# A hybrid S5 / RG-LRU / GLA block on one core: a new order of the first norm, a moved projection block, an earlier fill and a moved group of rests

## The chip, the cores and the metric

One Trainium2 chip, one core. Input and output are fp32. The time is device microseconds of one launch; the kernel before takes 1577.93 us (median of 3 runs, 1577.77 to 1577.96). The engines are called PE (TensorE, matmuls), DVE (VectorE), ACT (ScalarE), POOL (GpSimd) and SP (SyncE, which only issues DMAs).

## The reference, cut to what matters

```python
mod = split((silu(c) @ ada_w + ada_b), 6);  mod_c = the same of c_ctx
u  = modulate(rms_norm(x, ln1_g), mod[0], mod[1])        # 1024 latent tokens x 1024
uc = modulate(rms_norm(ctx, ln1_g), mod_c[0], mod_c[1])  # 256 context tokens x 1024
zl, zc = split(u @ w_in), split(uc @ w_in)               # 1024 x 5408
s5  = S5 scan (256 channels, two directions), gelu, GLU
lru = RG-LRU scan (256 channels, two directions, short conv), times gelu(g)
gla = chunked GLA: 4 heads, q, k of 64, v of 128, chunks of 64, two directions, RMSNorm, times silu(g)
m = sig(g0)*(s5 @ w_br_s5) + sig(g1)*(lru @ w_br_lru) + sig(g2)*(gla @ w_br_gla)
h = x + mod[2] * (m @ w_out)
u = modulate(rms_norm(h, ln2_g), mod[3], mod[4])
hid = dwconv3(u @ w_up)                                  # 1024 x 5632
h = h + mod[5] * ((silu(gate) * val) @ w_down)           # 2816 -> 1024
out = rms_norm(h, final_g)
```

The context goes only through the projection and starts the scans of the latent tokens.

## The kernel before, in words

Activations lie transposed: a tile is 128 channels by 512 or 1024 tokens. Each fp32 product is three matmuls of fp32r operands: high times high, rest times high, high times rest. So every operand is split: its high part is a rounded copy (`wh`, `uh`, `y0h`; mostly ACT) and its rest is the difference to that copy (`wl`, `ul`, `y0l`; DVE or POOL).

The work goes through these stages in time:

- **Start** (list `START`, L87, runs the small functions of class `Start`, L330 to L446). `x`, `sq`, `sa` load and square the eight tiles of x and add up the squares, for token half j = 0 or 1; `rs` sums over channels on PE (L285), `re`, `rp` give the reciprocal root (`rp` is the POOL power at L408), `rb` broadcasts it by PE (L279), `rc` copies it. `a` loads a piece of the adaLN weights, `ar` multiplies a row of eight such pieces (64 matmuls, L316), `at`, `ac`, `am` turn the row into shift and scale of two channel tiles. `un`, `u`, `ul` scale a tile by norm and scale (DVE, L320), add the shift and round (ACT, L323) and take the rest (DVE, L326). `g`, `gh`, `gl` load and split the first weights. `m1` and `m2` are the matmuls of three column blocks with the high part (L434, L435) and the rest (L441); `mz` the last of them. Each list entry issues in the order of the list on every engine.
- **The stream.** `proj_stream` (L762) is a generator of all further projection matmuls in the order in which they are to run. A block of 128 columns on the latent tokens (`lat`) is 48 matmuls of 128x512 in 8 steps of two rows of tokens, stored by the `out_rows` functions. `fill(us)` (L868) takes matmuls from the stream until their summed cost reaches the given number; `F(name)` takes the number from the table `FILL` (L62). The mixers' own matmuls stand between such calls, so the stream fills the time in which a mixer waits. Blocks of the stream share two PSUM buffers each of `ma` and `mb`; ACT or DVE copies them out (the v blocks at L746).
- **LRU, S5, GLU** (L950 to L1260), then **four GLA heads** (class `Head`, L1294; driver at L1488). Of the heads, number 0 makes its decays (L1304 to L1323, DVE and ACT), and then PE transposes (L1347). After the last head `fill(1e9)` (L1531) empties the stream; its last blocks are the gated products, whose gates are added at L826 and L827.
- **Merge** (L1540 to L1580): the heads' output is written to DRAM as `yosp` (L1434), read back as `yr` in four tiles through two buffers (`wide_in`, L1549), split into `y0h`, `y0l` to `y3h`, `y3l`, and multiplied with the branch weights in eight products of 24 matmuls (L290 to L292). Weights come through `wblock`: two raw buffers `wr`, three `wh`, three `wl`.
- **Output projection, residual, second norm**, then the **up projection** in pairs of hidden blocks by a Strassen-like scheme (class `Pair`, L1629): products p1 to p7 of the four quarters of the activation and of sums of them. At the turn from the norm to the pairs (L1790 to L1925) the operand differences T1 to T4 and the quarter B22 are made tile by tile: `sub` (difference, L1831), `hi` (ACT copy, L1834), `lo` (rest, L1837). `units(k)` issues the products 5, 7 and 6 of both first pairs for tile k; p3 multiplies with B22, p4 with T4; `c57` and `z57` add earlier products up before p3 and p4 write to the same PSUM banks. The order of DVE, ACT, POOL and PE is by hand there.
- **Down projection** and the final norm.

The order of PE is as the code is written (`manual_schedule`). In the start and at the turn the other engines are by hand too; elsewhere a scheduler orders them, SP included.

Of the kernel before, what the change touches and what calls it, by code (L numbers as in the profile page):

```python
# [12 lines left out]
OP = mybir.AluOpType  # L13
# [7 lines left out]
KT = 8  # L21
# [16 lines left out]
def _parts(v, bits, n):  # L38
    out = []
    for _ in range(n):  # L40
# [69 lines left out]
def tile_kernel(tc, I, out, dbg=None):  # L110
# [154 lines left out]
    def t0(shape, tag, bufs=1):  # L265
        return p0_.tile(list(shape), F32, name=nm("t0"), tag=tag, bufs=bufs)
# [64 lines left out]
    class Start:  # L331
# [65 lines left out]
        @staticmethod
        def rs(j):
# [482 lines left out]
    def F(name):  # L881
        fill(next(fills[name]))
# [612 lines left out]
    G.memset(Tm, 0.0)  # L1495
    for h in range(4):
        if h == 0:
            F("gtr")
            head.transposed()
            F("gds")  # L1500
            head.states()
        nxt = Head(h + 1) if h < 3 else None
        head.scores(0)

        if nxt:
            with tc.issue_after(head.last.ins):
# [827 lines left out]
```

## Time and profile before

| | |
|---|---|
| median of 3 runs | 1577.93 us |
| profiled execution | 1578.69 us |
| its span, first to last instruction | 1576.6 us |
| PE busy | 1513.6 us, 96% of the span |
| DVE busy | 1096.1 us, 70% |
| ACT busy | 772.3 us, 49% |
| POOL busy | 414.6 us, 26% |
| mean granted TensorE clock | 0.985 |

Busy time is time in which an engine executes. PE is the busiest by far; the span less its busy time is its idle time. The clock is granted at two levels, 2.4 GHz (1.00) and 1.2 GHz (0.50), and a mean between them tells how much of a stretch ran at the lower one. A 128x512 matmul follows its predecessor by 0.23 us at the higher level and by 0.43 us at the lower. A "wait" is idle time of an engine just before an instruction, with the engine and line that released it.

### The profile page before, as it was taken

To read this page: it belongs to the slowest core of one execution; us is meant where nothing else is said; L and a number is where in the kernel's file an instruction comes from. 1 tells how busy PE (TensorE), PEld (TensorE's weight loads), DVE (VectorE), ACT (ScalarE), POOL (GpSimd) and SP (SyncE) were. 2 spreads that over 40 slices of the span, in tenths; PEclk is the share of its full clock that TensorE was granted. 3 is DMA by queue.
4 is the path that set the end of the run, shared out by engine and by line. 5 is a ranking of instruction groups with operands and counts; after the bars stand their busy time and mean duration, and the time that the engine had idled before them with its cause. 6 is when DMAs were issued, how large, how long until landed. Compare 5 with 4: busy or idle time off the path is not lost. (4 is left out here: it accounts for less than half of the span.)

```text
span 1576.6 us, 21571 instructions
## 1 busy us (share of the span) xinstructions
PE 1513.6 (96%) x8144; PEld 1248.9 (79%) x8144; DVE 1096.1 (70%) x1645; ACT 772.3 (49%) x1223; POOL 414.6 (26%) x266
## 2 busy tenths in 40 slices
PE   5999989999996999999999989999999999999997
PEld 4788768877885888888888867778888888878887
DVE  3624379999858434642451899888888888899962
ACT  4523776785534543441332565444444444544661
POOL 2313210011124222222236335333333333000032
PEclk9999999999998999999999999999999999999998
DMA  9764533332224244131574411222222223964303
GB/s 327 256 213 132 187 129 105 117 101 59 59 67 134 77 135 148 70 88 63 172 239 145 141 60 54 94 81 80 81 81 83 93 92 109 371 240 141 101 20 107
DMA packets 93865, 199.04 MB, mean 126 GB/s; under 512 B 13505, under 2 KB 34881, under 8 KB 93633
## 3 DMA queue, kind: packets, MB, share of 16 engines
q1 hardware_dynamic: 82048, 181.75, 34.3%
q10 hardware_dynamic: 11712, 15.91, 2.9%
q8 instruction: 64, 1.05, 0.3%
q14 instruction: 41, 0.33, 0.1%
HBM read 159.11 MB, written 38.52 MB: 125 GB/s over the span
## 5 line engine op out<-in xcount | busy, mean ns | idle before, releaser
L221 POOL TENSOR_TENSOR wl<-wr,wh 128x1024 fp32r<-128x1024 f32 (+1 forms) x78 | 164.2, 2105 | 477.1 <-ACT wh L220 432.8
L220 ACT CAST wh<-wr 128x1024 fp32r<-128x1024 f32 (+2 forms) x87 | 77.1, 891 | 146.2 <-issue 41.3
L221 POOL TENSOR_TENSOR wp<-tmp,wp 128x512 fp32r<-128x512 f32 x44 | 75.2, 1726 | 217.6 <-ACT wp L220 217.6
L534 PE MATMUL ma<-uh,wh 128*128 128x512 f32 x272 | 116.9, 430 | 0.7 <-ACT pt L809 0.7
L534 PE MATMUL mb<-uh,wh 128*128 128x512 f32 x272 | 106.7, 392 | 0.0
L536 PE MATMUL ma<-ul,wh 128*128 128x512 f32 x272 | 106.7, 392 | 0.0
L536 PE MATMUL mb<-ul,wh 128*128 128x512 f32 x272 | 106.7, 392 | 0.0
L538 PE MATMUL mb<-uh,wl 128*128 128x512 f32 x272 | 106.2, 391 | 0.0
L538 PE MATMUL ma<-uh,wl 128*128 128x512 f32 x272 | 105.9, 389 | 0.0
L220 ACT CAST wp<-tmp 128x512 fp32r<-128x512 f32 x78 | 46.5, 619 | 91.4 <-DVE tmp L1648 91.2
L1714 DVE SCALAR_TENSOR_TENSOR ca<-gv,vec,ca 128x1023 f32<-128x1023 f32 (+2 forms) x66 | 62.2, 967 | 23.8 <-ACT ca L1706 23.6
L220 ACT CAST wp<-hd 128x512 fp32r<-128x512 f32 x88 | 52.8, 618 | 49.4 <-PE bkd L2023 26.3
L220 ACT CAST wp<-wr 128x512 fp32r<-128x512 f32 x97 | 58.2, 620 | 32.5 <-DMA wr<-in_wdn_dram 17.1
L1717 DVE SCALAR_TENSOR_TENSOR ca<-gv,vec,ca 128x1023 f32<-128x1023 f32 (+2 forms) x66 | 71.1, 1100 | 0.1
L1378 DVE SCALAR_TENSOR_TENSOR gl<-gl,gl 128x128 f32<-128x128 f32 x72 | 31.2, 433 | 53.1 <-ACT gl L1376 35.6
L534 PEld LDWEIGHTS ma<-uh,wh 128*128 128x128 f32 x272 | 51.3, 189 | 15.4 <-issue 5.2
L221 DVE TENSOR_TENSOR wp<-hd,wp 128x512 fp32r<-128x512 f32 x88 | 60.8, 708 | 1.2 <-ACT wp L220 1.0
L538 PEld LDWEIGHTS ma<-uh,wl 128*128 128x128 f32 x272 | 51.2, 188 | 11.3
L536 PEld LDWEIGHTS ma<-ul,wh 128*128 128x128 f32 x272 | 51.2, 188 | 11.3
L536 PEld LDWEIGHTS mb<-ul,wh 128*128 128x128 f32 x272 | 51.2, 188 | 11.2
L538 PEld LDWEIGHTS mb<-uh,wl 128*128 128x128 f32 x272 | 51.1, 188 | 11.4
L534 PEld LDWEIGHTS mb<-uh,wh 128*128 128x128 f32 x272 | 51.4, 189 | 9.6 <-issue 1.4
(643 smaller groups left out, 4606.3 us busy)
## 6 DMA issues: line engine op xcount, KB each, us to landing
wa<-in_ada_dram SPq DMA_DIRECT2D x96, 256.0 KB
wr<-in_wup_dram SPq DMA_DIRECT2D x46, 512.0 KB
wr<-in_win_dram SPq DMA_DIRECT2D x40, 512.0 KB
wr<-in_wdn_dram SPq DMA_DIRECT2D x22, 512.0 KB
hd<-hid SPq DMA_DIRECT2D x22, 512.0 KB
hid<-ca SPq DMA_DIRECT2D x21, 512.0 KB
wr<-in_wout_dram SPq DMA_DIRECT2D x16, 512.0 KB
tmp<-in_wdn_dram SPq DMA_DIRECT2D x22, 256.0 KB
```

The source lines that it names most:

```text
L220: S.copy(h, src)
L221: lo.tensor_tensor(l, src, f32(h), OP.subtract)
L534: PE.matmul(p[j], h[:, kk], uh[j][:, k], start=f, stop=False)
L536: PE.matmul(p[j], h[:, kk], ul[j][:, k], start=False, stop=False)
L538: PE.matmul(p[j], l[:, kk], uh[j][:, k], start=False, stop=e)
L1378: self.last = V.scalar_tensor_tensor(Sd[:, step], Sd[:, step - 1], self.dec[:, step:step + 1], Sd[:, step], OP.mult, OP.add)
L1714: V.scalar_tensor_tensor(a[:, t0_ + 1:t0_ + 1 + n1], x[:, o:o + n1], fw[0], a[:, t0_ + 1:t0_ + 1 + n1], OP.mult, OP.add)
L1717: V.scalar_tensor_tensor(a[:, t0_ + c - 1:t0_ + n - 1], x[:, o + c:o + n], fw[2], a[:, t0_ + c - 1:t0_ + n - 1], OP.mult, OP.add)
```

## The change

It has four parts.

1. `START` has a new order. The row of adaLN weights is split: its first six pieces are multiplied as soon as they are there, for row 0 ahead of the norm's broadcast, and the last two later. `u(0,0)` and `u(1,0)` stand ahead of the later squares of the second half. The rows 1 to 3 of the weights come earlier among `m1` and `m2`. Three adds of squares go from POOL to DVE, and the third square has a buffer of its own.
2. In the stream, the second q block (`qsp[1]`, 8 steps, 48 matmuls) goes from ahead of the context blocks to behind the first v steps, just ahead of the steps of z.
3. A new cost `gtr0` of 13.0 is filled from the stream ahead of head 0's transposes. It takes 60 matmuls (10 steps); so many fewer are left behind the last head.
4. At the turn, the last two copies and the four rests of B22 go from behind the difference work to right behind the last rest of T2, the rests from POOL to DVE. q[1].p3 goes ahead of q[0].p4 with its gate and output.

```diff
-ONPOOL = [('sq', 2, 1), ('sq', 4, 1), ('sq', 6, 1)]
...
+        'gtr0': [13.0],
...
-    def ada_rows(r, p):
-        for k, w in enumerate(ada.pop(r)):
+    def ada_rows(r, p, k0=0, k1=KT):
+        for k in range(k0, k1):
+            w = ada[r][k]
...
-                t = sqs[k, j] = t0([128, 512], "sq", 3)
+                t = sqs[k, j] = t0([128, 512], "sq" if k != 2 else "sqp", 3 if k != 2 else 1)
...
-            (G if ("sq", k, j) in ONPOOL else V).tensor_tensor(accs1[j], accs1[j], sqs[k, j], OP.add)
+            V.tensor_tensor(accs1[j], accs1[j], sqs[k, j], OP.add)
...
-        wsrc.extend([win[i] for i in (35, 36, 37, 0, 5, 6, 3, 4)] + vsrc)
+        wsrc.extend([win[i] for i in (35, 36, 37, 0, 5, 3, 4)] + vsrc + [win[6]])
...
-        for b in range(2):
-            yield from lat(lambda p: out_rows(p, qsp[b]))
+        yield from lat(lambda p: out_rows(p, qsp[0]))
         for b in range(2):
             yield from ctx(lambda p: out_rows([p], ksp[b]))
         yield from v_steps([0, 1])
+        yield from lat(lambda p: out_rows(p, qsp[1]))
         yield from z_steps()
...
         if h == 0:
+            F("gtr0")
             F("gtr")
             head.transposed()
...
     lo(2, 3)
+    hi(5, 2); hi(5, 3)
+    for k in range(4):
+        lo(5, k)
     units(3)
...
-    hi(5, 2); hi(5, 3)
     for k in range(4):
-        lo(5, k, G)
         sub(4, k)
...
     nxt.sums((7, 3))
+    q[1].p3()
     q[0].p4()
     q[0].gate()
     q[0].out()
-    q[1].p3()
     q[1].p4()
```

On ACT in the start, where L391 (L392 after) are squares, L323 (L324) the first two `u` of half 0, and `t_139` the broadcast norm, there stood before:

```order
L416 COPY t_139<-sm_131 128x512
L377 CAST wh_137<-wr_202 128x256
L391 ACTIVATE t_243<-x_89 128x512
L391 ACTIVATE t_247<-x_90 128x512
L391 ACTIVATE t_253<-x_91 128x512
L391 ACTIVATE t_257<-x_92 128x512
L391 ACTIVATE t_264<-x_93 128x512
L391 ACTIVATE t_268<-x_94 128x512
L391 ACTIVATE t_272<-x_95 128x512
L323 ACTIVATE uh_109<-x_89,mods 128x512
L323 ACTIVATE uh_109<-x_90,mods 128x512
L391 ACTIVATE t_286<-x_96 128x512
```

and now:

```order
L378 CAST wh_137<-wr_222 128x256
L392 ACTIVATE t_233<-x_89 128x512
L392 ACTIVATE t_237<-x_90 128x512
L426 COPY t_139<-sm_131 128x512
L392 ACTIVATE t_251<-x_91 128x512
L324 ACTIVATE uh_109<-x_89,mods 128x512
L324 ACTIVATE uh_109<-x_90,mods 128x512
L392 ACTIVATE t_273<-x_92 128x512
L392 ACTIVATE t_276<-x_93 128x512
L392 ACTIVATE t_283<-x_94 128x512
```

The two `u` stood behind seven squares of the second half; now they stand behind three.

On SP around the last head's output, where `wr` are raw branch weights for the merge, `acc` a weight piece for the up projection and `tg` stored products, there stood before:

```order
L211 DMA wr_6774<-in_wbr_dram 128x256
L1434 DMA yosp<-gl_6512 128x1024
L211 DMA wr_6892<-in_wbr_dram 128x512
L1863 DMA acc_8093<-in_wup_dram 128x512
L1549 DMA yr_6904<-yosp 128x1024
L1549 DMA yr_6908<-yosp 128x1024
L1549 DMA tg_6925<-tsp 128x1024
L1549 DMA tg_6964<-tsp 128x1024
L1549 DMA yr_6912<-yosp 128x1024
L211 DMA wr_6898<-in_wbr_dram 128x512
L1549 DMA yr_6916<-yosp 128x1024
```

and now:

```order
L211 DMA wr_6759<-in_wbr_dram 128x256
L211 DMA wr_6892<-in_wbr_dram 128x512
L211 DMA wr_6898<-in_wbr_dram 128x512
L211 DMA wr_6951<-in_wbr_dram 128x512
L1444 DMA yosp<-gl_6596 128x1024
L1874 DMA acc_8093<-in_wup_dram 128x512
L1560 DMA yr_6904<-yosp 128x1024
L1560 DMA yr_6908<-yosp 128x1024
L1560 DMA tg_6925<-tsp 128x1024
L1560 DMA tg_6964<-tsp 128x1024
L1560 DMA yr_6912<-yosp 128x1024
L1560 DMA yr_6916<-yosp 128x1024
```

`yosp` stood ahead of all three weight loads of the merge; now it stands behind them. The last two `yr` have no weight load between them any more.

At the turn POOL had, before:

```order
L221 TENSOR_TENSOR wp_8044<-tmp_8011,wp_8044 128x512
L221 TENSOR_TENSOR wp_8212<-pt_7868,wp_8212 128x512
L221 TENSOR_TENSOR wp_8215<-acc_8093,wp_8215 128x512
L1837 TENSOR_TENSOR B22l<-h_7281,B22h 128x512
L1837 TENSOR_TENSOR B22l<-h_7283,B22h 128x512
L1837 TENSOR_TENSOR B22l<-h_7285,B22h 128x512
L1837 TENSOR_TENSOR B22l<-h_7287,B22h 128x512
L221 TENSOR_TENSOR wp_8265<-pt_8015,wp_8265 128x512
```

and now DVE has, where `wr_8099` begins the sums of the third pair's weights:

```order
L1848 TENSOR_TENSOR T3l<-h_7279,T3h 128x512
L1848 TENSOR_TENSOR T2l<-h_7279,T2h 128x512
L1848 TENSOR_TENSOR B22l<-h_7281,B22h 128x512
L1848 TENSOR_TENSOR B22l<-h_7283,B22h 128x512
L1848 TENSOR_TENSOR B22l<-h_7285,B22h 128x512
L1848 TENSOR_TENSOR B22l<-h_7287,B22h 128x512
L1659 TENSOR_TENSOR tmp_8194<-wr_8099 128x512
L1659 TENSOR_TENSOR tmp_8196<-tmp_8194,wr_8097 128x512
L221 TENSOR_TENSOR wp_8198<-wr_8097,wp_8198 128x512
L221 TENSOR_TENSOR wp_8201<-tmp_8196,wp_8201 128x512
```

The four rests of B22 stood on POOL behind two rests of weights; now they stand on DVE between the rests of T2 and those sums, and POOL has nothing in their place.

## Rows read from the trace of the kernel before

**Rows 1.** The page: busy us, share of the span, instructions.

```profile
PE 1513.6 (96%) x8144; PEld 1248.9 (79%) x8144; DVE 1096.1 (70%) x1645; ACT 772.3 (49%) x1223; POOL 414.6 (26%) x266
```

**Rows 2.** Waits of PE: who waited for whom, us in total, times, longest.

```profile
PE sm L1347 <- DVE gl L1323: 12.6, 1, 12.6
PE ma L434 <- ACT uh L323: 4.9, 1, 4.9
PE mb L711 <- ACT pt L746: 4.8, 1, 4.8
...
PE sm L1260 <- DVE s L1245: 1.7, 2, 1.3
```

**Rows 3.** Windows: busy us of the engines in a stretch, clock, DMA share, GB/s.

```profile
20.00:40.00 20.00, 14.52 (x196) 12.06 (x187) 9.45 (x20) 6.95 (x14) 6.91 (x7) 0.83 0.91 323
40.00:60.00 20.00, 19.07 (x139) 15.36 (x140) 19.93 (x30) 10.04 (x18) 8.65 (x7) 1.00 0.95 342
200.00:220.00 20.00, 15.22 (x85) 11.28 (x84) 18.30 (x15) 14.31 (x17) 2.14 (x1) 0.83 0.59 198
```

**Rows 4.** Timeline of PE from 12 to 40 us: start, duration, line, idle before, releaser.

```profile
15.85 2.07 PE L279 MATMUL sm<-con,t 128*128 128x128 f32 x8 [1.35 <-POOL t L408]
17.85 3.64 PE L316 MATMUL sm<-wa,c 128*32 128x128 f32 x64
27.26 0.80 PE L434 MATMUL ma<-uh,wh 128*128 128x512 f32 x1 [4.86 <-ACT uh L323]
...
34.74 1.95 PE L316 MATMUL sm<-wa,c 128*32 128x128 f32 x64
```

**Rows 5.** Timeline of ACT from 19 to 33 us.

```profile
26.50 1.32 ACT L323 ACTIVATE uh<-x,mods 128x512 fp32r<-128x512 f32 x2
```

**Rows 6.** Timeline of ACT, then of PE, from 204 to 222 us.

```profile
215.06 0.57 ACT L746 COPY pt<-mb 128x512 f32<-128x512 f32 x1
...
215.68 0.69 PE L711 MATMUL mb<-uh,tmp 128*64 128x512 f32 x1 [4.78 <-ACT pt L746]
```

**Rows 7.** Timeline of PE from 494 to 516 us.

```profile
496.70 0.39 PE L538 MATMUL mb<-uh,wl 128*128 128x512 f32 x1
509.74 2.39 PE L1347 MATMUL sm<-con,gl 128*128 128x128 f32 x10 [12.65 <-DVE gl L1323]
511.78 0.77 PE L534 MATMUL ma<-uh,wh 128*128 128x512 f32 x1
...
```

**Rows 8.** Timeline of SP, DVE and PE from 738 to 778 us.

```profile
740.17 1.95 PE L279 MATMUL sm<-con,gl 128*128 128x128 f32 x16
...
744.71 0.33 SPq L1434 DMA_DIRECT2D yosp<-gl  x1
...
747.83 0.90 SPq L1549 DMA_DIRECT2D yr<-yosp  x2
...
754.42 1.23 DVE L221 TENSOR_TENSOR y0l<-yr,y0h 128x1024 fp32r<-128x1024 f32 x1 [7.81 <-ACT y0h L220]
...
758.17 0.37 SPq L1549 DMA_DIRECT2D yr<-yosp  x1
...
764.79 1.23 DVE L221 TENSOR_TENSOR y3l<-yr,y3h 128x1024 fp32r<-128x1024 f32 x1 [2.12 <-ACT y3h L220]
...
770.78 0.39 PE L290 MATMUL mm<-y0h,wh 128*128 128x512 f32 x1
```

**Rows 9.** Window of half a us, the last with data behind the issue of yosp.

```profile
746.50:747.00 0.50, 0.50 (x4) 0.41 (x3) 0.11 (x1) 0.00 (x0) 0.44 (x1) 1.00 0.62 246
```

**Rows 10.** Timeline of POOL, DVE and PE at the turn, 930 to 962 us.

```profile
938.58 0.68 DVE L221 TENSOR_TENSOR wp<-wr,wp 128x512 fp32r<-128x512 f32 x1
...
942.94 6.84 POOL L1837 TENSOR_TENSOR B22l<-h,B22h 128x512 fp32r<-128x512 f32 x4
...
945.15 1.78 DVE L1837 TENSOR_TENSOR T4l<-h,T4h 128x512 fp32r<-128x512 f32 x1
...
953.48 0.47 PE L853 MATMUL bkd<-T4h,wp 128*128 128x512 f32 x1 [3.15 <-DVE gv L1688]
```

More of the change, by code (lines that the diff above doesn't have):

```diff
@@ L85 @@
 ENGS = {mybir.EngineType.DVE, mybir.EngineType.Pool, mybir.EngineType.Activation, mybir.EngineType.SP}
-ONPOOL = [('sq', 2, 1), ('sq', 4, 1), ('sq', 6, 1)]
-START = [('x', 0, 0), ('sq', 0, 0), ('x', 1, 0), ('sq', 1, 0), ('x', 2, 0), ('sq', 2, 0), ('sa', 1, 0), ('x', 3, 0), ('sq', 3, 0), ('sa', 2, 0), ('x', 4, 0), ('sq', 4, 0), ('sa', 3, 0), ('x', 5, 0), ('sq', 5, 0), ('sa', 4, 0), ('x', 6, 0), ('sq', 6, 0), ('sa', 5, 0), ('x', 7, 0), ('sq', 7, 0), ('sa', 6, 0), ('sa', 7, 0), ('rs', 0), ('re', 0), ('rp', 0), ('rb', 0), ('a', 0, 0), ('a', 0, 1), ('a', 0, 2), ('a', 0, 3), ('a', 0, 4), ('a', 0, 5), ('a', 0, 6), ('a', 0, 7), ('g', 0), ('gh', 0, 0), ('gh', 0, 1), ('ar', 0), ('gl', 0, 0), ('rc', 0), ('gl', 0, 1), ('gh', 0, 2), ('x', 0, 1), ('sq', 0, 1), ('gl', 0, 2), ('x', 1, 1), ('sq', 1, 1), ('at', 0), ('ac', 0), ('x', 2, 1), ('sq', 2, 1), ('sa', 1, 1), ('x', 3, 1), ('sq', 3, 1), ('am', 0), ('sa', 2, 1), ('x', 4, 1), ('sq', 4, 1), ('un', 0, 0), ('x', 5, 1), ('sq', 5, 1), ('un', 1, 0), ('x', 6, 1), ('sq', 6, 1), ('u', 0, 0), ('sa', 3, 1), ('u', 1, 0), ('ul', 0, 0), ('m1', 0, 0), ('sa', 4, 1), ('x', 7, 1), ('sq', 7, 1), ('ul', 1, 0), ('sa', 5, 1), ('m2', 0, 0), ('m1', 1, 0), ('sa', 6, 1), ('sa', 7, 1), ('m2', 1, 0), ('rs', 1), ('a', 1, 0), ('a', 1, 1), ('a', 1, 2), ('a', 1, 3), ('a', 1, 4), ('a', 1, 5), ('a', 1, 6), ('a', 1, 7), ('g', 1), ('gh', 1, 0), ('ar', 1), ('re', 1), ('gh', 1, 1), ('rp', 1), ('gh', 1, 2), ('gl', 1, 0), ('rb', 1), ('at', 1), ('gl', 1, 1), ('gl', 1, 2), ('ac', 1), ('rc', 1), ('am', 1), ('un', 0, 1), ('un', 1, 1), ('u', 0, 1), ('a', 2, 0), ('a', 2, 1), ('a', 2, 2), ('a', 2, 3), ('a', 2, 4), ('a', 2, 5), ('a', 2, 6), ('a', 2, 7), ('ar', 2), ('un', 2, 0), ('u', 1, 1), ('ul', 0, 1), ('g', 2), ('gh', 2, 0), ('u', 2, 0), ('gl', 2, 0), ('m1', 0, 1), ('ul', 1, 1), ('gh', 2, 1), ('gh', 2, 2), ('at', 2), ('gl', 2, 1), ('ul', 2, 0), ('ac', 2), ('gl', 2, 2), ('un', 3, 0), ('m2', 0, 1), ('m1', 1, 1), ('am', 2), ('u', 3, 0), ('un', 2, 1), ('ul', 3, 0), ('m1', 2, 0), ('u', 2, 1), ('un', 3, 1), ('a', 3, 0), ('a', 3, 1), ('a', 3, 2), ('a', 3, 3), ('a', 3, 4), ('a', 3, 5), ('a', 3, 6), ('a', 3, 7), ('ar', 3), ('ul', 2, 1), ('u', 3, 1), ('un', 4, 0), ('g', 3), ('gh', 3, 0), ('gh', 3, 1), ('gl', 3, 0), ('ul', 3, 1), ('gh', 3, 2), ('m2', 1, 1), ('u', 4, 0), ('gl', 3, 1), ('at', 3), ('un', 5, 0), ('m2', 2, 0), ('gl', 3, 2), ('ul', 4, 0), ('ac', 3), ('u', 5, 0), ('m1', 3, 0), ('am', 3), ('ul', 5, 0), ('m1', 2, 1), ('un', 4, 1), ('un', 5, 1), ('u', 4, 1), ('m2', 3, 0), ('un', 6, 0), ('u', 5, 1), ('m2', 2, 1), ('ul', 4, 1), ('u', 6, 0), ('m1', 3, 1), ('ul', 5, 1), ('ul', 6, 0), ('m1', 4, 0), ('un', 7, 0), ('un', 6, 1), ('m2', 3, 1), ('u', 7, 0), ('un', 7, 1), ('m2', 4, 0), ('u', 6, 1), ('ul', 7, 0), ('m1', 5, 0), ('u', 7, 1), ('ul', 6, 1), ('m1', 4, 1), ('ul', 7, 1), ('m2', 5, 0), ('m2', 4, 1), ('m1', 5, 1), ('m1', 6, 0), ('m2', 5, 1), ('m2', 6, 0), ('m1', 6, 1), ('m2', 6, 1), ('mz',)]
@@ new lines @@
+START = [('x', 0, 0), ('sq', 0, 0), ('x', 1, 0), ('sq', 1, 0), ('x', 2, 0), ('sq', 2, 0), ('sa', 1, 0), ('x', 3, 0), ('sq', 3, 0), ('sa', 2, 0), ('x', 4, 0), ('sq', 4, 0), ('sa', 3, 0), ('x', 5, 0), ('sq', 5, 0), ('sa', 4, 0), ('x', 6, 0), ('sq', 6, 0), ('sa', 5, 0), ('x', 7, 0), ('sq', 7, 0), ('sa', 6, 0), ('sa', 7, 0), ('rs', 0), ('a', 0, 0), ('a', 0, 1), ('a', 0, 2), ('a', 0, 3), ('a', 0, 4), ('a', 0, 5), ('ar', 0, 0, 6), ('re', 0), ('rp', 0), ('a', 0, 6), ('a', 0, 7), ('g', 0), ('gh', 0, 0), ('rb', 0), ('gh', 0, 1), ('gl', 0, 0), ('gh', 0, 2), ('x', 0, 1), ('sq', 0, 1), ('gl', 0, 1), ('x', 1, 1), ('sq', 1, 1), ('gl', 0, 2), ('ar', 0, 6, 8), ('rc', 0), ('sa', 1, 1), ('x', 2, 1), ('sq', 2, 1), ('at', 0), ('ac', 0), ('sa', 2, 1), ('am', 0), ('un', 0, 0), ('un', 1, 0), ('u', 0, 0), ('u', 1, 0), ('ul', 0, 0), ('m1', 0, 0), ('ul', 1, 0), ('x', 3, 1), ('sq', 3, 1), ('x', 4, 1), ('sq', 4, 1), ('sa', 3, 1), ('m2', 0, 0), ('x', 5, 1), ('sq', 5, 1), ('m1', 1, 0), ('sa', 4, 1), ('x', 6, 1), ('sq', 6, 1), ('sa', 5, 1), ('x', 7, 1), ('sq', 7, 1), ('a', 1, 0), ('a', 1, 1), ('a', 1, 2), ('a', 1, 3), ('a', 1, 4), ('a', 1, 5), ('ar', 1, 0, 6), ('sa', 6, 1), ('sa', 7, 1), ('m2', 1, 0), ('a', 1, 6), ('a', 1, 7), ('g', 1), ('gh', 1, 0), ('gh', 1, 1), ('gl', 1, 0), ('ar', 1, 6, 8), ('gh', 1, 2), ('rs', 1), ('at', 1), ('gl', 1, 1), ('gl', 1, 2), ('ac', 1), ('re', 1), ('rp', 1), ('am', 1), ('a', 2, 0), ('a', 2, 1), ('a', 2, 2), ('a', 2, 3), ('a', 2, 4), ('a', 2, 5), ('ar', 2, 0, 6), ('un', 2, 0), ('un', 3, 0), ('u', 2, 0), ('rb', 1), ('u', 3, 0), ('ul', 2, 0), ('a', 2, 6), ('a', 2, 7), ('g', 2), ('gh', 2, 0), ('ul', 3, 0), ('gh', 2, 1), ('gl', 2, 0), ('gh', 2, 2), ('ar', 2, 6, 8), ('rc', 1), ('gl', 2, 1), ('m1', 2, 0), ('at', 2), ('un', 0, 1), ('gl', 2, 2), ('un', 1, 1), ('u', 0, 1), ('ac', 2), ('m2', 2, 0), ('un', 2, 1), ('u', 1, 1), ('a', 3, 0), ('a', 3, 1), ('a', 3, 2), ('a', 3, 3), ('a', 3, 4), ('a', 3, 5), ('ar', 3, 0, 6), ('am', 2), ('u', 2, 1), ('ul', 0, 1), ('m1', 0, 1), ('ul', 1, 1), ('ul', 2, 1), ('a', 3, 6), ('a', 3, 7), ('g', 3), ('gh', 3, 0), ('gh', 3, 1), ('ar', 3, 6, 8), ('gl', 3, 0), ('un', 3, 1), ('gh', 3, 2), ('m2', 0, 1), ('gl', 3, 1), ('at', 3), ('u', 3, 1), ('un', 4, 0), ('m1', 1, 1), ('gl', 3, 2), ('ul', 3, 1), ('u', 4, 0), ('ac', 3), ('un', 5, 0), ('m2', 1, 1), ('am', 3), ('u', 5, 0), ('m1', 3, 0), ('ul', 4, 0), ('ul', 5, 0), ('m1', 2, 1), ('un', 4, 1), ('un', 5, 1), ('u', 4, 1), ('m2', 3, 0), ('un', 6, 0), ('u', 5, 1), ('m2', 2, 1), ('ul', 4, 1), ('u', 6, 0), ('m1', 3, 1), ('ul', 5, 1), ('ul', 6, 0), ('m1', 4, 0), ('un', 7, 0), ('m2', 3, 1), ('un', 6, 1), ('u', 7, 0), ('m2', 4, 0), ('un', 7, 1), ('u', 6, 1), ('m1', 5, 0), ('ul', 7, 0), ('u', 7, 1), ('ul', 6, 1), ('m1', 4, 1), ('ul', 7, 1), ('m2', 5, 0), ('m2', 4, 1), ('m1', 5, 1), ('m1', 6, 0), ('m2', 5, 1), ('m2', 6, 0), ('m1', 6, 1), ('m2', 6, 1), ('mz',)]
@@ L340, in ar @@
         @staticmethod
-        def ar(r):
-            ada_rows(r, psm[:, r * 128:(r + 1) * 128])
+        def ar(r, k0, k1):
+            ada_rows(r, psm[:, r * 128:(r + 1) * 128], k0, k1)
         @staticmethod
@@ L394, in sa, with sp, sf @@
         def sa(k, j):
-            (G if ("sq", k, j) in ONPOOL else V).tensor_tensor(accs1[j], accs1[j], sqs[k, j], OP.add)
+            V.tensor_tensor(accs1[j], accs1[j], sqs[k, j], OP.add)
+        @staticmethod
+        def sp(k, j):
+            G.tensor_tensor(sqs[2, j], sqs[2, j], sqs[k, j], OP.add)
+        @staticmethod
+        def sf(j):
+            Start.sa(2, j)
         @staticmethod
```

## The prediction

> **What bounds the kernel now.** I read the busy table first, then PE's waits, then the windows around the longest of them, and last the timelines inside those windows. PE is busy 1513.6 us of a span of 1576.6 us [rows 1], so 63 us of idle time, and the time that matmuls lose at the lower clock, are all that an edit of the order can win. The change adds no matmul and takes none away. PE's waits name the places that it touches: 12.6 us ahead of head 0's transposes, 4.9 us ahead of the first `m1`, 4.8 us in z [rows 2], and at the turn 3.15 us on PSUM buffer `bkd` [rows 10]. The clock costs time beside each: 0.83 of full speed in the windows 20 to 40 and 200 to 220 us [rows 3]. So I cost four parts apart, each at its own stage, against the profiled execution's 1578.69 us (2.1 us more than its span, 0.76 us above the median of 1577.93).
>
> **A. The start.** Before, the broadcast waits 1.35 us for POOL's power and ends at 17.9 us; the row of adaLN weights runs behind it to 21.5 us; the first `m1` begins at 27.26 us after 4.86 us of waiting [rows 4]. What it waits for is `u` on ACT at 26.50, which follows squares of the second half, some of them fed by POOL adds [rows 5]. After, the row's first six pieces (six eighths of 3.64, 2.7 us) begin right behind the sums at 14.5 and cover the power; the broadcast follows to 19.3, the last two pieces (0.9 us) to 20.2. The steps between row and `un` took 2.4 us before and the two `u` no longer stand behind four of the squares, so I put the first `m1` at about 23.2: 4.1 us earlier. Behind it PE's work is the same. A further 1.4 us I expect from the later rows, which now stand among `m1` and `m2`: at full clock such a row takes 1.95 us [rows 4] and its slots for loads come free sooner with less to wait for. That gives 5.5. Against it DVE is 19.93 of 20 us busy from 40 to 60 us [rows 3] and gets three more adds (some 2 us), though it has 10 us free from 20 to 40. I take -5, with bounds of -1 (only the broadcast's wait goes, everything else ends with the loads) and -7 (all of 4.86 and 1.35, and the clock rises sooner).
>
> **B. The moved q block.** The first matmul of z into the second `mb` buffer waits 4.78 us for ACT's copy of the last v block, which comes at 215.06, queued behind ACT's LRU work; the window has a clock of 0.83 [rows 3, 6]. At 0.43 us apart in place of 0.23, the some 4.8 us of matmuls behind the wait lose about 2.3 us. After, 48 matmuls (10.9 us) stand between the v copies and z, so the copy is long done. What is late next: z's second buffer then waits for the q block's own copies, which stand behind ACT's same chain; I find between 0 and 1.5 us for it, and at worst the whole 4.8. The full gain would be 7.1. I take -4, because LRU's chain on DVE (18.30 of 20 us busy from 200 to 220) must follow if PE is not to wait for it later; bounds 0 and -7.
>
> **E. The fill ahead of head 0.** 126 matmuls of the stream run from 742.1 to 770.78 [rows 8], 0.2277 us each, so 60 are 13.66 us. PE's work ends at 497.09 and the transposes begin at 509.74 [rows 7], 12.65 us later. So the wait is covered, with 1.0 us over; the transposes (10 in 2.04 us) and the first five matmuls behind them run at the lower clock before, and cost 2 us less at the higher. Net the transposes' end is about 1.0 us earlier, and 13.66 us of stream are gone from the end: -14.7 if nothing follows.
>
> Something does follow. Let T be 742.1, the end of the last broadcast [rows 8]. Before, the first merge begins at T+28.7 and its 24 matmuls end at T+34.2; y3's rest is ready at 766.02, T+23.9, so it waits for nothing. After, 66 matmuls (15.05 us) are left, and the merge could begin at T+15. Its operands can't: `yosp` is issued at T+2.6 before, and three weight loads now stand ahead of it on SP, the last of which needs the first one's slot; I put it at T+3.75. The first `yr` was issued 3.1 us behind `yosp` [rows 8]. Data of that write were moving until about 746.9, 2.2 us behind its issue [rows 9], so the read comes 2.2 to 3.1 us behind it, at T+5.95 to T+6.85. From `yr` to the end of y0's rest took 7.8 us, and to that of y3's 18.2, of which 1.1 was a weight load ahead of the last `yr` that is now gone: y0 at T+14.7, y2 about T+21.5, y3 at T+23.1 to T+24. A quarter of a merge product is 1.37 us. The first two run on time, the third waits 3.7 us, the fourth ends at T+24.5 at best, and at T+27.8 with the later read and the lower clock behind the wait. Against T+34.2 that is -6.4 to -9.7, with head 0's -1.0 it is -7.4 to -10.7. I take -8; the outer bounds are -5 and -14.7.
>
> The trace can't say which ended the wait of `yr`, the write's end or the queue. The Trainium skill, "DMA: Bandwidth & Descriptors", on where a transfer's fixed cost goes, says a transfer's semaphore fires only when its last byte is confirmed, some 2.0 us plus bytes at 436 GB/s; for 512 KB that is an estimate of 3.2 us, and the trace's 3.1 agrees. By that rule the read comes at T+6.95, and E is near -7.5; by the queue alone, at T+4.5, it would be near -10.
>
> **C and D. The turn.** POOL makes the four rests of B22 from 942.94 in 6.84 us. Beside them four DVE operations took 1.78 each, such as a rest of T4 at 945.15; the same size takes 0.68 otherwise [rows 10]. On DVE the four rests cost 4 x 0.6 (spacing of such operations) = 2.4 us, and save up to 4 x 1.1 = 4.4; the net of -2 moves up q[0]'s last sum, whose absence makes PE wait 3.15 us ahead of p4, and half clock follows. The 2.4 us come ahead of the third pair's sums, so its weights are that much later. With q[1].p3 (12 matmuls, 2.7 us) ahead of q[0].p4, PE has work in that wait if q[1]'s own sums and weights are ready; POOL makes those, and is freed earlier. I find about 1.4 us of wait left in place of 3.15. I take -2; bounds 0 (DVE, which runs without a gap beside these rests, hands the 2.4 us on to PE) and -4.5.
>
> **The sum.** -5 -4 -8 -2 = -19: 1578.69 - 19 = 1559.7 in the profiled execution's terms, 1559 in the median's. The bounds add to -6 and -33.
>
> **The rivals.**
>
> - *The merge gives E back.* The stream runs dry at T+15 and PE waits for y2, y3 and then the merge's weights, which SP issues only behind the `yr`; the half clock stretches the products. For it: y3 is 8.9 us behind the merge's earliest start. Against it: two weights stand ahead of `yosp`, and before the merge ran without a gap. E is then 0: 1567.
> - *DVE sets the pace.* In the stages behind the start and behind z, DVE is 18 to 20 of 20 us busy [rows 3], and neither A nor B takes anything from it. Then A and B vanish into waits for DVE: -10, 1568. Against it: PE waits on DVE nowhere between z and head 0 for more than 1.3 us at once, in S5 at L1260 [rows 2], so DVE has some room there.
> - *Slower: SP holds `yosp`.* The third weight load waits for the slot of the first, freed by POOL's rest, which needs a free `wl` among three that the stream's blocks use. If that comes only when the stream's last block ends (T+15), `yosp` goes out at T+17.4, `yr` at T+20.5, y3 is ready at T+37.6, and the first merge ends at T+39, with the lower clock about T+41.5 in place of T+34.2: E is +6.3. With the other parts at their low ends (-1) that is +5: 1583. It decides from the point where the load waits past T+14. For it: the scheduler put the loads ahead. Against it: the slot's block is used up at about T+1.4.
> - *The change doesn't bite.* Each wait finds another releaser at the same time (loads in the start, ACT's copies in z, head 0's decays later because ACT and DVE copy out the filled blocks): within 3 us of 1578.
>
> **How the numbers follow.** What a measurement can tell from no change is 0.2%, 3.2 us. Forecast 0.59; merge gives E back 0.14; DVE sets the pace 0.14; SP holds `yosp` 0.07, of which slower 0.06 and faster 0.01; no bite 0.05, which is the same; anything else slower 0.01. Faster is then 0.59 + 0.14 + 0.14 + 0.01 = 0.88, the same 0.05, slower 0.07. The range is 1547 (12 below the forecast, with most parts near their best bound) to 1573 (14 above: either middle rival and a further 5 us, or a part of both).
>
> **What would show it.** The wait at L1347 gone, and PE at a clock of 1.00 from 490 to 515 us. The first `m1` at about 23 us and the start's end five to six us earlier. The wait at L711 gone or under 1.5 us. A new wait of 3 to 7 us in the first merge (L290 or L291, on y2 or y3). At the turn, rests of T4 at 0.68 and a `bkd` wait near 1.4. Wrong would be: a merge that waits over 10 us, `yosp` later than T+6, or a stage between 70 and 480 us that gets a DVE wait as long as what the start gained.

## The result, and the profile after

The changed kernel takes 1553.55 us (median of 4 runs, 1552.12 to 1554.15) against 1577.95 us: a ratio of 0.9843, interval 0.9826 to 0.9860, so 24.4 us faster. A second set of runs gave 1552.99 us and 0.9846 (0.9833 to 0.9860). Forecast were 1559 us and a range of 1547 to 1573. Below, a kernel's distance to the changed one is its ratio less 0.9845 (between the two ratios just named), times 1577.7 us. Each ratio's interval is about ±0.0014, or ±2.2 us, and a distance holds two of them, so about ±3 us.

First the page, to set beside [rows 1] (engines' busy time and share):

```profile
PE 1508.3 (97%) x8144; PEld 1240.7 (80%) x8144; DVE 1090.7 (70%) x1652; ACT 773.6 (50%) x1223; POOL 398.5 (26%) x259
```

The span is 1552.4 us. PE is idle for 44 us in place of 63, and its busy time is 5 us less with the same 8144 matmuls: the mean clock is 0.996 in place of 0.985.

The waits of PE after (who waited for whom, us in total, times, longest), to set beside [rows 2]:

```profile
...
PE ma L444 <- ACT uh L324: 2.0, 1, 2.0
PE sm L317 <- DMA wa<-in_ada_dram: 1.7, 7, 0.3
...
PE bkd L863 <- DVE gv L1699: 1.4, 1, 1.4
...
PE mm L290 <- ACT y2h L220: 1.3, 1, 1.3
...
PE mm L291 <- DVE y2l L221: 0.8, 1, 0.8
```

The wait ahead of head 0 and the one in z are gone, the first `m1`'s has shrunk to 2.0 us. New are PE's waits for weight pieces in the start and for y2 in the merge. The wait of 1.4 us on `bkd` is not the one at the turn: it comes at 990.9 us, in a later pair.

The windows after (busy us by engine, then clock, DMA share, GB/s), the first three beside [rows 3]:

```profile
20.00:40.00 20.00, 16.38 (x217) 11.43 (x217) 14.36 (x27) 9.20 (x18) 6.54 (x7) 1.00 1.05 387
40.00:60.00 20.00, 19.81 (x107) 15.91 (x108) 18.52 (x30) 10.18 (x19) 5.96 (x4) 1.00 1.00 349
200.00:220.00 20.00, 19.50 (x143) 13.16 (x142) 13.35 (x11) 18.25 (x24) 2.40 (x1) 1.00 0.32 116
480.00:520.00 40.00, 39.85 (x219) 32.79 (x218) 22.68 (x23) 19.41 (x34) 16.35 (x7) 1.00 0.24 83
748.00:756.00 8.00, 6.47 (x19) 4.53 (x20) 3.85 (x4) 2.29 (x3) 1.12 (x1) 0.79 0.26 96
```

The clock is 1.00 where it was 0.83; of the stretches shown, only the first merge's lost it.

Where did the time come from? The same matmuls found in both traces tell how much earlier each place comes: behind the start -4.2 us, behind z and from there to head 0 -11.7, at the last head's broadcast -12.5, behind the first merge -21.9, at 935 us (behind the turn's third products) -25.2, at the end -24.8. So by these two executions the parts are A -4.2, B -7.5, E -10.2 (-0.9 at head 0, -9.4 at the merge) and C with D -2.9.

The timeline of PE in the start after (start, duration, line, idle before and releaser), beside [rows 4]:

```profile
14.24 2.79 PE L317 MATMUL sm<-wa,c 128*32 128x128 f32 x48
16.96 1.30 PE L279 MATMUL sm<-con,t 128*128 128x128 f32 x8
18.18 0.64 PE L317 MATMUL sm<-wa,c 128*32 128x128 f32 x16
20.08 0.39 PE L352 MATMUL sm<-con,t 128*128 128x8 f32 x2 [1.25 <-DVE t L348]
22.49 0.50 PE L444 MATMUL ma<-uh,wh 128*128 128x512 f32 x1 [2.02 <-ACT uh L324]
...
30.95 0.42 PE L317 MATMUL sm<-wa,c 128*32 128x128 f32 x8 [0.25 <-DMA wa<-in_ada_dram]
31.62 0.43 PE L317 MATMUL sm<-wa,c 128*32 128x128 f32 x8 [0.25 <-DMA wa<-in_ada_dram]
...
35.74 0.50 PE L444 MATMUL ma<-uh,wh 128*128 128x512 f32 x1
```

Six pieces run in the time of POOL's power, as intended, and the first `m1` is at 22.49, 4.8 us earlier. Behind it the lead first grows to 7.1 us, because these matmuls follow each other 0.23 us apart, and before 0.43. But the third row's pieces come one by one, 0.67 us apart, and behind the start 4.2 us are left.

At head 0 (timeline of PE, beside [rows 7]) the transposes follow the stream without a gap and at the higher clock:

```profile
498.95 0.39 PE L548 MATMUL mb<-uh,wl 128*128 128x512 f32 x1
499.18 1.25 PE L1357 MATMUL sm<-con,gl 128*128 128x128 f32 x10
500.19 0.48 PE L544 MATMUL ma<-uh,wh 128*128 128x512 f32 x1
```

The tail after, from the timeline of all engines, beside [rows 8]:

```profile
727.63 1.95 PE L279 MATMUL sm<-con,gl 128*128 128x128 f32 x16
...
733.16 0.33 SPq L1444 DMA_DIRECT2D yosp<-gl  x1
...
734.00 1.55 SPq L1560 DMA_DIRECT2D yr<-yosp  x2
...
741.61 1.05 ACT L220 CAST y0h<-yr 128x1024 fp32r<-128x1024 f32 x1 [10.40 <-DMA yr<-yosp]
...
742.69 1.23 DVE L221 TENSOR_TENSOR y0l<-yr,y0h 128x1024 fp32r<-128x1024 f32 x1 [7.63 <-ACT y0h L220]
...
743.94 1.56 SPq L1560 DMA_DIRECT2D yr<-yosp  x2
...
744.50 0.39 PE L290 MATMUL mm<-y0h,wh 128*128 128x512 f32 x1
...
748.68 0.50 PE L290 MATMUL mm<-y2h,wh 128*128 128x512 f32 x1 [1.27 <-ACT y2h L220]
...
750.00 0.50 PE L291 MATMUL mm<-y2l,wh 128*128 128x512 f32 x1 [0.82 <-DVE y2l L221]
...
750.74 1.23 DVE L221 TENSOR_TENSOR y3l<-yr,y3h 128x1024 fp32r<-128x1024 f32 x1 [0.80 <-ACT y3h L220]
...
753.89 0.63 PE L292 MATMUL mm<-y3h,wl 128*128 128x512 f32 x1
...
754.32 0.51 PE L290 MATMUL mm<-y0h,wh 128*128 128x512 f32 x1
```

With T at 729.58, `yosp` goes out at T+3.6, the merge begins at T+14.9, y2's rest is ready at T+20.4 and y3's at T+22.4, and the first product ends at T+24.7 in place of T+34.2.

At the turn (timeline of all engines, beside [rows 10]) the rests of B22 cost 2.49 us and those of T4 0.68 each, in place of 1.78:

```profile
915.36 2.49 DVE L1848 TENSOR_TENSOR B22l<-h,B22h 128x512 fp32r<-128x512 f32 x4
...
924.62 0.68 DVE L1848 TENSOR_TENSOR T4l<-h,T4h 128x512 fp32r<-128x512 f32 x1
...
929.33 0.49 PE L863 MATMUL bkc<-B22h,wp 128*128 128x512 f32 x1 [0.94 <-ACT gv L1695]
...
930.10 0.50 PE L864 MATMUL bkc<-B22h,wp 128*128 128x512 f32 x1 [0.28 <-POOL wp L221]
```

### The profile page after: what moved, and what is told of

Read it like the earlier page. It is cut to its first block, busy times and chain, and to the rows that moved or that the text cites. A ratio compares the mean times of both kernels' runs of the same rounds, so it can differ in the third digit from the quotient of the medians.

```text
span 1552.4 us, 21567 instructions
## 1 busy us (share of the span) xinstructions
PE 1508.3 (97%) x8144; PEld 1240.7 (80%) x8144; DVE 1090.7 (70%) x1652; ACT 773.6 (50%) x1223; POOL 398.5 (26%) x259
## 5 line engine op out<-in xcount | busy, mean ns | idle before, releaser
L1725 DVE SCALAR_TENSOR_TENSOR ca<-gv,vec,ca 128x512 f32<-128x512 f32 (+2 forms) x66 | 61.0, 949 | 25.4 <-ACT ca L1717 25.0
L1728 DVE SCALAR_TENSOR_TENSOR ca<-gv,vec,ca 128x1023 f32<-128x1023 f32 (+2 forms) x66 | 69.7, 1081 | 0.1
```

Of the source, the lines that this page charges most:

```text
L1725: V.scalar_tensor_tensor(a[:, t0_ + 1:t0_ + 1 + n1], x[:, o:o + n1], fw[0], a[:, t0_ + 1:t0_ + 1 + n1], OP.mult, OP.add)
L1728: V.scalar_tensor_tensor(a[:, t0_ + c - 1:t0_ + n - 1], x[:, o + c:o + n], fw[2], a[:, t0_ + c - 1:t0_ + n - 1], OP.mult, OP.add)
```

## The experiments

All times are medians; "before" ran beside each set.

**Each part undone.** Four kernels, each the changed one with one part put back.

```diff
 e1: START, ada_rows, ar, sq and sa as before
 e2: qsp[1] back behind qsp[0], its weights too
 e3: no gtr0
 e4: the turn as before
```

> The changed kernel with the start as before (part A undone). Theory (the parts add up; in the trace A moves everything behind the start by -4.2 us): 4.2 us slower than the changed kernel, 1557.8 us, and the later places shift by that same 4.2. Rival (the start's gain is only visible there, and a later stage would have given it back or made it up without A): within 1 us of the changed kernel's 1553.6. Second rival (A also prepares B, since both move the load queue): 7 us or more slower, 1560 or more.

> The changed kernel with the second q block back ahead of the context blocks (part B undone). Theory: the wait of some 4.8 us in z for ACT's copy returns, with the lower clock behind it, and all of the -7.5 us that the trace shows between the start and S5 is B's: 1561.0 us. Rival (VectorE's LRU chain sets the pace behind z, so an earlier z only waits later): 0 to 2 us slower, 1554 to 1555.5. Second rival (part of the -7.5 is A's, since the copies of v come earlier with it): 4 to 6 us, 1558 to 1560.

> The changed kernel without the fill ahead of head 0 (part E undone). Theory: the wait of 12.6 us ahead of head 0's transposes returns with its lower clock, the merge waits for nothing, and the total is 10.2 us slower than the changed kernel, 1563.8 us. Rival (the stream's shortening gives all of it back, and the difference of the traces at the merge comes from elsewhere): under 3 us slower. Full value without the merge's wait would be 14.7 us, 1568.

> The changed kernel with the turn as before (parts C and D undone). Theory: the rests of T4 take 1.78 us again beside POOL, the wait of 3.15 us on PSUM buffer bkd returns, and it is 2.9 us slower, 1556.5 us. Rival (the turn's wait is made up by the later pairs): under 1 us.

| undone | us | ratio to before | to the changed kernel |
|---|---|---|---|
| A | 1554.70 | 0.9855 (0.9842 to 0.9869) | +1.6 |
| B | 1559.72 | 0.9885 (0.9872 to 0.9899) | +6.3 |
| E | 1565.63 | 0.9924 (0.9911 to 0.9936) | +12.5 |
| C and D | 1555.07 | 0.9858 (0.9843 to 0.9873) | +2.1 |

They add to 22.5 of 24.4 us, so within these intervals the parts add up. B and E stand clear of them; the 1.6 of A and the 2.1 of C and D do not. For these the traces decide, by the same matmuls as above. Behind the start e1 is 1.9 us ahead of the kernel before, and the eleven other traces (that of the run without loads, below, apart) are 3.3 to 4.4 ahead. From 898 to 964 us of the kernel before, across the turn, e4 loses 1.0 us, and the ten traces with C and D in them gain 3.3 to 3.4. A was undone only as a whole, so which of its steps gives the gain isn't shown. With B undone the old wait stands there again, and with E undone the other (waits of PE of the two kernels):

```profile
PE mb L721 <- ACT pt L756: 4.8, 1, 4.8
```

```profile
PE sm L1356 <- DVE gl L1332: 12.6, 1, 12.6
```

What was won in z is not given back on the way to head 0: the same matmuls of e2 and of the changed kernel stay 6.4 us apart from 210 to 588 us. That is against the rival in which DVE sets the pace there. E comes out larger than the -10.2 of the two traces, A smaller than -4.2.

A first. With the old start in e1, the start ended 1.9 us earlier than with the same start in the kernel before. Its timeline of PE, to set beside [rows 4], shows why:

```profile
17.68 2.78 PE L317 MATMUL sm<-wa,c 128*32 128x128 f32 x64
...
25.97 0.80 PE L444 MATMUL ma<-uh,wh 128*128 128x512 f32 x1 [4.70 <-ACT uh L324]
```

The row took 2.78 us in place of 3.64: the clock rose within it. The wait ahead of `m1` is nearly the same. So by these two traces about half of A's -4.2 belongs to when the clock rose in the profiled execution of before, and A itself is near -2.

As for E, the second profile of the changed kernel has the end of the first merge product at T+22.1 in place of T+24.7. Its timeline of all engines, with T at 729.83, to set beside the tail above:

```profile
740.35 1.05 ACT L220 CAST y0h<-yr 128x1024 fp32r<-128x1024 f32 x1 [8.89 <-DMA yr<-yosp]
...
746.26 1.06 ACT L220 CAST y2h<-yr 128x1024 fp32r<-128x1024 f32 x1 [1.11 <-DMA yr<-yosp]
...
748.69 0.50 PE L291 MATMUL mm<-y2l,wh 128*128 128x512 f32 x1 [0.80 <-DVE y2l L221]
...
750.69 0.51 PE L291 MATMUL mm<-y3l,wh 128*128 128x512 f32 x1 [0.35 <-DVE y3l L221]
```

`yosp` and the first `yr` were issued at the same places (T+3.6 and T+4.4), but the first tile was there for ACT at T+10.5 in place of T+12.0. So y2, whose read needs y0's buffer, was there earlier too. PE waited 1.2 us in place of 2.1, and its clock is 1.00 from 748 to 756 us, where it was 0.79 in the first profile. Of the 2.6 us, about 0.9 are the waits and 1.7 the clock. Between 454 and 797 us of the kernel before, E gives -10.1 to -13.5 us in the eight traces with the full fill and two read buffers; with E undone it is +0.1, and undoing E gave 12.5. Sixteen completions are recorded for that first read; fifteen were there by T+10.6 and T+10.4, and the last came at T+12.0 and T+10.5. So in the first profile one of them was late, and why is open.

**Loads in the start.** A third row without loads:

```diff
     def ada_part(r, k):
+        if r == 2:
+            ada[r] = ada[0]
+            return
```

> The changed kernel without the loads of the adaLN weights' third row (8 of 256 KB); its matmuls take the first row's weights, so that part of shift and scale is wrong. Theory (behind the first matmul the start is paced by its loads; the row's pieces came 0.67 us apart, and PE waited for them): the waits of PE for weight pieces go, the start's end comes 3 to 5 us earlier, and the total falls by as much, to 1549 to 1550.5. Rival (VectorE's or PE's own work sets the start's end): the waits go, the end stays within 1 us, 1553.6.

1551.46 us, ratio 0.9831 (0.9817 to 0.9846). The waits for pieces went, but the start's end moved by only -0.6 us, not by -3 to -5; in the trace the rest of the difference lies at the merge, where the first tile was there at T+10.0. Windows of its start, beside the changed kernel's:

```profile
20.00:24.00 4.00, 1.81 (x5) 1.47 (x6) 3.84 (x10) 2.20 (x4) 0.00 (x0) 0.62 1.05 386
24.00:28.00 4.00, 4.00 (x11) 3.16 (x10) 3.34 (x5) 1.91 (x4) 0.00 (x0) 0.53 1.05 390
28.00:32.00 4.00, 4.00 (x75) 2.78 (x74) 0.29 (x1) 1.02 (x3) 1.88 (x3) 1.00 0.52 150
```

```profile
20.00:24.00 4.00, 1.90 (x9) 1.54 (x10) 3.84 (x10) 2.28 (x4) 0.00 (x0) 1.00 1.05 387
24.00:28.00 4.00, 4.00 (x60) 3.13 (x59) 3.26 (x5) 1.83 (x4) 0.00 (x0) 1.00 1.05 388
28.00:32.00 4.00, 3.50 (x53) 2.14 (x51) 1.89 (x7) 1.02 (x3) 1.95 (x3) 1.00 1.05 387
```

Without the loads PE worked without a gap behind the first wait, at the lower clock at first (0.62, 0.53); with them it ran at the higher clock and waited. Both end within 0.6 us. In nine other traces of the changed start the first `m1` and `m2` ran at the lower clock too, in whole or in part. They were 0.9 to 2.4 us behind the changed kernel's first profile by 31 us, and yet the start's end came within 0.2 us of its: what the clock lost, the loads would have cost anyway. In e5 (four read buffers, below) it was 3.0 us behind by then, and the end came 0.9 us later. So two limits lie close together, and taking one away buys little. Higher clock without these loads was not seen.

**Half a fill, and where the other half goes.**

```diff
 e6: -        'gtr0': [13.0],
     +        'gtr0': [6.5],
 e9: the same, and
     -        'gsc': [13.0, 13.0, 12.0, 12.0],
     +        'gsc': [19.5, 13.0, 12.0, 12.0],
```

> The changed kernel with a fill of 6.5 in place of 13.0 ahead of head 0 (30 matmuls, 6.83 us). Theory (each filled us is one us of the wait, until the merge waits for y2 and y3): about 5.8 us of the wait and the lower clock behind it stay, the merge waits for nothing, E is about -6.8 in place of -10 to -12, so 1557 to 1559. Rival (the gain is that of the clock and of the wait going as a whole, so half of a fill gives little): 1562 or more.

> The changed kernel with the fill ahead of head 0 at 6.5 (30 matmuls) and head 0's score fill at 19.5 in place of 13.0, so that the other 30 matmuls run a little later and the stream meets the heads 1 to 3 and the merge as in the changed kernel. Theory (the half fill lost its gain because the stream's blocks met the later heads at another point, where PE waited 4.8 and 2.0 us for ScalarE's copies of gates behind a head's chain): those waits are gone, about 6 us of the wait ahead of head 0 and some 2 us of lower clock remain, 1560 to 1562.5. Rival (the amount filled ahead of head 0 decides, and the wait left there puts the heads out of step with the copies): the waits for ScalarE's copies stay, 1565 or more.

Half a fill took 1566.39 us (0.9930, 0.9918 to 0.9942): as slow as none, though PE's wait ahead of head 0 fell from 12.6 to 6.0 us. The theory of one us for each filled us fell, and the rival's reason is not the right one either. The trace of e6 has two waits for ACT's copies of gates, of 4.8 and 2.0 us, where the changed kernel and e3 have none over 0.8. They take back the 6.6 us that half the fill won. The timeline of all engines at the first:

```profile
644.70 0.22 ACT L1321 ACTIVATE gl<-gl 64x20 f32<-64x20 f32 x1 [3.68 <-DVE gl L1317]
...
645.69 0.60 ACT L819 ACTIVATE pt<-ma 128x512 f32<-128x512 f32 x1
...
646.34 0.79 PE L544 MATMUL ma<-uh,wh 128*128 128x512 f32 x1 [4.81 <-ACT pt L819]
```

ACT holds the copy of a finished gate behind a step of the next head's decays, which waits for DVE; the stream needs that buffer. By 30 matmuls the stream's blocks had slid against the heads. With the other 30 put back ahead of head 1 (e9), both waits are gone, the wait of 5.9 us ahead of head 0 stays, and the time is 1561.60 us (0.9902), as expected.

**Four read buffers.**

```diff
-        t = pyp.tile([128, 1024], F32, name=nm(name), tag=name, bufs=2)
+        t = pyp.tile([128, 1024], F32, name=nm(name), tag=name, bufs=4 if name == "yr" else 2)
```

> The changed kernel with four buffers in place of two for the tiles in which the heads' output is read back, so that all four reads go out behind each other. Theory (what the fill lost at the end is the wait for y2 and y3, which can't be read before y0's and y1's buffers are free): the third and fourth tile are ready about 4 and 2 us sooner, the waits of 1.3 and 0.8 us in the first merge go, its matmuls keep the higher clock, and the total falls by 2 to 4 us, to 1550 to 1551.5. Rival (the merge waits for the first read or for its weights, and the buffers don't matter): no change, 1553.6. Second rival (four reads at once slow the first two down): the merge begins later, 1 us slower.

> The changed kernel as it is, beside the next one on the same chip: 1552 to 1554.

> Four read buffers, as once before. Theory: 1.5 to 3 us faster than the changed kernel on the same chip, 1550 to 1552. Rival (the first comparison was chance): within 1 us of it.

1551.34 us (0.9835, 0.9820 to 0.9850) in the first set, 1553.09 (0.9849, 0.9836 to 0.9863) in the second, beside 1552.99 for the changed kernel. The waits for y2 go and one of 1.1 us for y3's rest stays; behind the merge the second set's trace is 0.6 us ahead of the changed kernel's second profile, whose own waits there add to only 1.2 us. What holds y3 now is DVE: ACT's copy of y3 ends at T+16.3, but DVE makes four operations of the stream's last gates (L836, L837) first and begins y3's rest at T+19.2. No gain that these runs can tell, so no version here beats the changed kernel clearly.

**C and D apart.**

> The changed kernel with the four rests of B22 back on GpSimd behind the difference work; q[1].p3 stays ahead of q[0].p4. Theory (the gain at the turn is VectorE's, which no longer runs beside GpSimd): rests of T4 take 1.78 us again, q[1].p3 finds its operands late or PE waits some 2 to 3 us, 1555 to 1556.5. Rival (the new order of p3 and p4 alone covers the wait): no slower than the changed kernel, 1553.6.

> The changed kernel with q[0].p4, its gate and output back ahead of q[1].p3; the rests of B22 stay on VectorE. Theory (the rests on VectorE carry the turn's gain, and the order of p3 and p4 only covers what is left of the wait): PE waits 1 to 1.5 us for the last sum ahead of q[0].p4, 1554 to 1556. Rival (C and D are worth nothing alone and need each other; C undone alone came out at 1558.7): 1557 or more.

With the rests back on POOL and q[1].p3 still first (C undone): 1558.73 us, 0.9881 (0.9862 to 0.9900), five runs from 1554.18 to 1562.99 us. With the old order of p3 and p4 (D undone): 1553.76 us, 0.9852. In e8 two rests of T4 beside POOL's rests take 1.78 us again and PE waits ahead of q[1].p3 in place of q[0].p4 (timeline of all engines):

```profile
921.16 1.78 DVE L1848 TENSOR_TENSOR T4l<-h,T4h 128x512 fp32r<-128x512 f32 x1
...
929.17 0.50 PE L863 MATMUL bkc<-B22h,wp 128*128 128x512 f32 x1 [2.83 <-ACT gv L1695]
```

Across the turn, as above, the trace with D undone gains 3.5 us, that with C undone nothing. So C carries the turn's gain; D adds about 1 us by the times, which these intervals can't tell from none, and D without C gives no gain there. The profile with C undone is that of the fastest of the five runs, with a mean clock of 0.993; the other four have 0.989 to 0.990. Why they lost more is open.

## Why the prediction was right

The sign, the range and the four mechanisms were right; the sum, 19, was 5 us short of 24.4. B and E were too small and A too large, so part of the errors cancelled, which is luck. Two of the signs named did not come: the first merge did not wait 3 to 7 us, and the start's end was not five to six us earlier but 4.2.

- **A, -5, too large.** Mechanism as told: the pieces covered POOL's power, the first `m1` came at 22.5 (23.2 forecast). What failed is the step "a further 1.4 us I expect from the later rows": between the first `m1` and the start's end the lead shrank from 4.8 to 4.2 us, where the third row's pieces come 0.67 us apart and PE waits for them. Undoing A gave 1.6 us, and by e1's trace about half of the -4.2 was the clock of the profiled execution of before.
- **B, -4, too small.** The q block's own copies, which I held against it, made no wait, and DVE took nothing back. The full value that I had named, 7.1, is what the trace gave (-7.5; 6.3 by undoing).
- **E, -8, too small.** Head 0 was as told (-0.9). At the end, y0's rest came at T+14.3 (T+14.7), y3's at T+22.4 (T+23.1 to T+24). The mis-sized term is "y2 about T+21.5", from which the wait of 3.7 us followed: y2's high part, with which PE begins, was there at T+19.0 and its rest at T+20.4, in the second profile at T+17.5 and T+18.8. So the first product ended at T+24.7 and T+22.1, near or ahead of the "T+24.5 at best". The lower clock behind the wait, which I put at the range's bad end, came in two of the eight traces with this merge. Undoing E gave 12.5.
- **The read behind `yosp`.** I took the 3.1 us from `yosp` to `yr` for the write's time or the queue's, and couldn't say which. The program could: `yosp` has a tile for each head, the first `yr` reads head 0's, which was written some 150 us earlier, and only y3's read needs the last write. And so could the trace of before: a weight load stood between the two on SP, and it went out when POOL had made the rest that frees its buffer (timeline of all engines, before):

```profile
744.26 2.68 POOL L221 TENSOR_TENSOR wl<-wr,wh 128x1024 fp32r<-128x1024 f32 x1 [4.45 <-ACT wh L220]
...
746.97 0.33 SPq L211 DMA_DIRECT2D wr<-in_wbr_dram  x1
```

So it was the queue, and that the estimate of 3.2 us agreed with it was chance. With no weight load between them, `yr` was issued at T+4.4, 0.84 us behind `yosp`: "by the queue alone, at T+4.5". The sum used T+5.95 to T+6.85, so the issue came 1.5 to 2.4 us earlier than that; but from the issue to y0's rest it took 9.9 us in the first profile and 8.4 in the second, in place of the 7.8 reckoned. The two errors nearly cancel in the first profile: that T+14.7 came near its T+14.3 is luck.

- **C and D, -2.** The rests of T4 took 0.68, and in place of 3.15 us ahead of q[0].p4 PE waited 0.94 and 0.28 ahead of q[1].p3, near the 1.4 forecast. By the traces -2.9, by undoing 2.1.
- **The rivals.** *The merge gives E back*: it waited 2.1 us for y2, in the second profile 1.2 for y2 and y3, not 9. *DVE sets the pace*: nothing came back between 216 and 490 us. *SP holds `yosp`*: the last weight load went out at T+3.0, when POOL's rest freed its buffer, and `yosp` at T+3.6, right behind DVE's last operation on its tile.

## What to carry to other kernels

A wait on one engine can be filled with work from the program's end, and pays as long as what follows the end is ready; but the amount also sets where a running stream meets every later stage, so half a fill can be worth nothing, and the waits of all later stages are to be read again. Where two limits lie close together, here the loads and the clock in the start, the profile of one execution names only one of them, and removing it buys the distance to the other. A gain read from two single executions holds chance in it, of the clock and of when a read lands: undo each part, time it, and compare the same place in every trace.

## What was not expected of the hardware

The clock at a given place differs from execution to execution of the same code. Of the twelve traces of the changed start, only the first profile's ran at 1.00 throughout the first `m1` and `m2`; in the others it was lower for some or all of them, behind the same wait of 2.0 us, and these matmuls followed each other by 0.43 us in place of 0.23. The landing of a read differs too: in ten traces with the same order on SP, the merge's first tile was there for ACT 5.6 to 7.9 us behind its read's issue. In the eight of them with two read buffers PE then waited 0.6 to 2.5 us in the merge; its clock fell there in two (waits of 2.1 and 2.5 us) and not in a third with 2.2. Of the kernel before, the runs shown beside the experiments go from 1575.47 to 1581.53 us.
